# Loads of the scan's operands, issued half by half from the sync engine's queue instead of in one burst from GpSimd's

## The chip, the cores and the metric

One core of a Trainium2 chip runs the whole program. The metric is the device time of one execution in microseconds (us). Engines are called as in the profile: PE is TensorE (PEld its weight loads), DVE is VectorE, ACT is ScalarE, POOL is GpSimd, SP is SyncE, which only issues DMAs. The granted clock of PE is given as a share of 2.4 GHz: 1.00 is 2.4 GHz, 0.50 is 1.2 GHz.

## The reference, cut to what matters

The program is a two-layer network on 256 latent and 256 context tokens, 1024 channels wide, all in float32. Layer 0 mixes tokens by a recurrence (RWKV-7), layer 1 by attention; each mixer stands between two half feed-forward blocks. The change touches the recurrence alone:

```python
def rwkv_scan(state0, dd, reverse):
    def step(s, inp):
        r_t, w_t, k_t, v_t, a_t, b_t = inp
        sa = jnp.einsum('bhvk,bhk->bhv', s, a_t)
        s = s * w_t[:, :, None, :] + sa[..., None] * b_t[:, :, None, :] + v_t[..., None] * k_t[:, :, None, :]
        return s, jnp.einsum('bhvk,bhk->bhv', s, r_t)
```

It runs for 16 heads of 64 channels, forwards and backwards, over the context and then over the latent tokens.

## The kernel before, in words

The products of all layers are made of three passes (whi, wlo: each float32 operand is split in two), and fill most of the time. The scan is a stage of its own in the middle, from about 748 to 1134 us of the profiled execution. The stage before it (`rwkv_project`) has written its operands to DRAM for each of KT = 8 groups `ct` of two heads: `far` (the rates and receptances, read into the tile `ar`), `fbk` (the two sorts of keys, tile `bk`), `fv` (values, tile `v`), `fpc` (decays per chunk, tile `pc`), `fgl` and `bg` (for the readout). Tokens are cut into chunks of 64; a group has 8 chunks in each direction, in two halves `hf` of four.

A group goes through `produce` (scores of `ar` against `bk`, line 949, tile `scp`, masked by DVE into `sc`; `keys`, which transposes `bk` on PE, line 993, tile `btp`; `values`, line 973, tile `vtp`), `solve` (a triangular inverse on DVE), `couple` (64 and 32 small matmuls at a time, lines 1050, 1072 and 1089, tile `cpl`), `scan` (the recurrence over chunks, lines 1152 to 1197) and `readout` (lines 1213 to 1249).

The order is written out by hand. Time is counted in hops; a group starts every P = 24 hops, and at `t` hops after its own start a group does what the table `plan` says: `FILL` gives the pieces of `produce` (s is a score, k a key, v a value; the first digit is the half), `SOLVE` 14, `COUPLE` 30 to 40, `SCAN` from 41. So in every period of 24 hops PE does scores (hops 0 to 5), the couple of the group before (6 to 16), keys and values (15 to 23), all with scan steps between. `tc.manual_schedule()` keeps each engine to this order of emission.

The loads are issued from POOL's queue (`ldq = nc.gpsimd`). Group c loads for group c + 1 at `BK=(6, 9)`: `pc`, `ar` and `bk` of half 0 and of half 1, 512 KB for each `ar` or `bk`; its own `v`, 256 KB a half, at `V=(8, 14)`. `load_scan` at hops 30 and 42 reads `ax` and `r` out of `far` again, in pieces of 256 bytes, and the readout loads `ldgl` and `ldbg`. POOL issues in order, and does little else. `ar` and `v` have two buffers (pool `e2`), one for each half; `bk` has four (pool `m4`), so two for each half. The first group's `ar` and `bk` are loaded from SP before the loop.

Each engine's own instructions come by DMA as well: the profile's queue 8 (kind "instruction") brings 16 KB at a time.

Of the kernel before, what the change touches and what calls it, by code (L numbers as in the profile page):

```python
# [8 lines left out]
F32 = mybir.dt.float32  # L9
# [8 lines left out]
KT = 8  # L18
# [46 lines left out]
def drain(*gens):  # L65
    for g in gens:
        for _ in g:
            pass
# [19 lines left out]
class Net:  # L88


    def __init__(self, ctx, tc, a):
        self.ctx, self.tc, self.nc, self.a = ctx, tc, tc.nc, a
        self.last = {}
        self.plan = dict(
            P=24, SOLVE=14, RATE=5, COUPLE=range(30, 41), SCAN=41,
            FILL={0: ("s000", "s001"), 1: ("s010",), 2: ("s011",), 3: ("s100", "s101"), 4: ("s110",), 5: ("s111",), 15: ("k00",),
                  16: ("v00",), 17: ("v01",), 19: ("k01",), 20: ("k10",), 21: ("k11",), 22: ("v10",), 23: ("v11",)},
            END={(0, 0): (5, (3, 3)), (0, 1): (5, (3, 3)), (1, 0): (5, (3, 3))}, WO=(4, 4), NI=(5, 5),
            FST=(1, 3), WAIT=16, RH=0, FB=16, CLEAR=(14, 18), AS=1, BK=(6, 9), V=(8, 14), LOADS=(30, 42), SS=(6, 18), BC=(10, 22))
        nc = self.nc  # L100
        self.res = ctx.enter_context(tc.tile_pool(name="res", bufs=1))
        self.dram = ctx.enter_context(tc.tile_pool(name="dram", bufs=1, space=DRAM))
        self.vec = self.res.tile([128, NV, KT], F32, name="vec")
        self.cst = self.res.tile([128, NC], F32, name="cst")
        self.ones = self.res.tile([128, 128], F32, name="ones")
        cv = self.res.tile([128, KT, 2], F32, name="cv")
        self.cs = self.res.tile([128, KT, 32], F32, name="cs")
        self.mod = [self.res.tile([128, NMOD, KT, 2], F32, name=f"mod{l}") for l in range(2)]
        self.epsn = self.res.tile([128, 1], F32, name="epsn")
        self.epsg = self.res.tile([128, 1], F32, name="epsg")  # L110
        self.xsp = self.dram.tile([128, 2, KT, CTX], F32, name="xsp")
        nc.sync.dma_start(out=cv, in_=a["cv"])
        nc.sync.dma_start(out=self.vec, in_=a["vec"])
        nc.sync.dma_start(out=self.cst, in_=a["cst"])
        nc.vector.memset(self.epsg, GN_EPS)
        nc.vector.memset(self.ones, 1.0)
        nc.vector.memset(self.epsn, EPS)
        nc.vector.memset(self.cs, 0.0)
        nc.scalar.activation(out=self.cs[:, :, 0:2], in_=cv, func=AF.Silu)
# [19 lines left out]
    def mods01(self, b):  # L139
# [3 lines left out]
        for k4 in range(4):  # L143
            pool = self.first if k4 in self.plan["FST"] else self.wraw
            w = pool.tile([128, 2, 4, 128], F32, tag="mw" if pool is self.first else "raw", name="mw")
# [740 lines left out]
    def rwkv_scan(self):  # L886
        nc, a, tc = self.nc, self.a, self.tc
        with ExitStack() as st:
            def pool(nm, n, **kw):
                return st.enter_context(tc.tile_pool(name=nm, bufs=n, **kw))  # L890

            e2 = pool("e2", 2)
            l2 = pool("l2", 2)
            m3, m1, m2, m4, m5 = (pool(f"m{i}", i) for i in (3, 1, 2, 4, 5))
# [3 lines left out]
            idn = cst[:, C_ID:C_ID + 128]  # L898
            mask = cst[:, C_MK:C_MK + 128].unsqueeze(1).to_broadcast([128, 4, 128])

            def load(ct, hf, ldq=nc.gpsimd):

                z = zs.setdefault(ct, {})
                if hf == 0:
                    z["pc"] = m5.tile([128, 2, 8], F32, tag="pc", name="pc")
                    ldq.dma_start(out=z["pc"], in_=self.fpc[ct])
                z["bk", hf] = m4.tile([128, 2, 4, 128], F32, tag="bk", name="bk")
                z["ar", hf] = e2.tile([128, 2, 4, 2, 64], F32, tag="ar", name="ar")
                ldq.dma_start(out=z["ar", hf].rearrange("p d c s i -> p (d c s i)"), in_=self.far[ct, :, hf].rearrange("p d x -> p (d x)"))
                ldq.dma_start(  # L910
                    out=z["bk", hf].rearrange("p d c x -> p (d c x)"), in_=self.fbk[ct, :, hf].rearrange("p c s i -> p (c s i)"))

            def load_v(ct, hf):
                z = zs[ct]
                z["v", hf] = e2.tile([128, 2, 4, 64], F32, tag="v", name="v")
                ldq.dma_start(out=z["v", hf], in_=self.fv[ct, :, hf].rearrange("p d (c i) -> p d c i", c=4))

            def load_scan(ct, hf):

                z = zs[ct]  # L920
                src = self.far[ct, :, hf].rearrange("p d (c s i) -> p d c s i", c=4, s=2)
                ax = z["ax", hf] = axs[hf]
                for h in range(2):
                    q = 64 * h
                    ldq.dma_start(
                        out=ax[q:q + 64].rearrange("p d c s i -> p (d c) s i")[:, :, 1 - h],
                        in_=src[q:q + 64].rearrange("p d c s i -> p (d c) s i")[:, :, 0])
                z["r", hf] = m2.tile([128, 2, 4, 64], F32, tag="r", name="r")
                ldq.dma_start(out=z["r", hf], in_=src[:, :, :, 1])
# [321 lines left out]
            zs, reads = {}, []  # L1251
            ldq = nc.gpsimd
# [9 lines left out]
            def clear(t, n):  # L1262
                nc.scalar.activation(
                    out=t.rearrange("p a b c -> p (a b c)" if n == 2048 else "p a b c d -> p (a b c d)").rearrange("p (a b) -> p a b", b=128),
                    in_=self.ones.unsqueeze(1).to_broadcast([128, n // 128, 128]), func=AF.Copy, scale=0.0)

            def adv(g, n=1):
                for _ in range(n):
                    try:
                        next(g)  # L1270
                    except StopIteration:
                        return False
                return True

            pl = self.plan
            live = []
            load(0, 0, nc.sync)
            load(0, 1, nc.sync)
            hop, P = 0, pl["P"]
            while hop < P * KT or live or reads:  # L1280
                ct, o = hop // P, hop % P
                if hop in pl["CLEAR"]:
                    i = pl["CLEAR"].index(hop)
                    clear(axs[i], 1024)
                    clear(tts[i], 2048)
                if o == 0 and ct < KT:
                    live.append([hop, ct, produce(ct), solve(ct), couple(ct), scan(ct)])
                for z in reversed(live[:]):
                    if hop - z[0] >= pl["SCAN"] and not adv(z[5]):
                        live.remove(z)  # L1290
                for t0, c, pr, so, co, sn in live:
                    t, z = hop - t0, zs[c]
                    late = list(z.get("late", ()))
                    if late:
                        z["late"].clear()
                    for f in late:
                        f()
                    if pl["SOLVE"] <= t < pl["COUPLE"][0]:
                        for _ in range(pl["RATE"]):
                            if next(so, True):  # L1300
                                break
                    if t == pl["COUPLE"][0]:
                        drain(so)
                    if t in pl["COUPLE"]:
                        adv(co)
                    for nm in pl["FILL"].get(t, ()):
                        pr(nm)
                    for hf in range(2):
                        if t == pl["BK"][hf] and c + 1 < KT:
                            load(c + 1, hf)  # L1310
                        if t == pl["V"][hf]:
                            load_v(c, hf)
                        if t == pl["LOADS"][hf]:
                            load_scan(c, hf)
                reads[:] = [g for g in reads if adv(g)]
                hop += 1
# [279 lines left out]
```

## Time and profile before

| | us |
|---|---|
| median of three runs | 2381.75 (2378.70 to 2394.33) |
| the profiled execution | 2379.8 |
| its span, first to last instruction | 2377.7 |
| PE busy | 2186.2 (92%) |
| DVE busy | 1515.8 (64%) |
| ACT busy | 1073.8 (45%) |
| POOL busy | 181.8 (8%) |

The span is the stretch from the first to the last instruction; 2.1 us of the execution's time lie around it. The groups below come from that one execution; their times count from the start of the span. The scan's periods can be told by the first score matmul (line 949) of each group, at 776.34, 810.44, 852.95, 896.99, 940.75, 985.56 and 1032.16 us for groups 1 to 7. In each period the stretch from the first `cpl` matmul to the `ss` matmuls of line 1225 is the couple, and what follows up to the next group's first score is the rest of keys and values.

### The profile page before, as it was taken

How to read it: one execution, taken by the hardware profiler on the slowest of the kernel's cores; microseconds unless marked ns; L12 is line 12 of the kernel's file. 1: busy time of each engine (PE TensorE's matmuls, PEld its weight loads, DVE VectorE, ACT ScalarE, POOL GpSimd, SP SyncE). 2: the span in 40 equal slices, each digit the busy share in tenths (PEclk: the TensorE clock that was granted, in tenths of full speed). 3: DMA queues.
4: the chain of work that ended last, by engine and by line, in shares of the span. 5: the costliest groups of instructions: out<-in, count | busy, mean ns of one | idle time of the engine just before them, and what ended most of it. 6: DMA issues, size and time to landing. Idle time of an engine off the chain costs nothing.

```text
span 2377.7 us, 44861 instructions
## 1 busy us (share of the span) xinstructions
PE 2186.2 (92%) x18548; PEld 1869.9 (79%) x18548; DVE 1515.8 (64%) x2609; ACT 1073.8 (45%) x1912; POOL 181.8 (8%) x273
## 2 busy tenths in 40 slices
PE   6999999888996789898899999999999999998997
PEld 4777889666674677677888788998878898678997
DVE  3798326576887666563689832479983367775554
ACT  3222235445884354454653222464222355555443
POOL 0000000000454223221000000000000000000000
PEclk9999999898997799889999999999999999798999
DMA  7677336442676433312567633567763364104664
GB/s 256 194 217 226 96 99 196 149 134 88 228 248 226 129 94 97 119 58 71 182 196 234 207 97 93 156 191 235 230 212 95 107 182 126 61 11 123 180 180 138
DMA packets 103051, 366.25 MB, mean 154 GB/s; under 512 B 13008, under 2 KB 15424, under 8 KB 100160
## 3 DMA queue, kind: packets, MB, share of 16 engines
q1 hardware_dynamic: 85536, 300.35, 40.7%
q0 software_dynamic: 17312, 63.05, 8.2%
q8 instruction: 145, 2.38, 0.4%
q14 instruction: 58, 0.48, 0.1%
HBM read 330.78 MB, written 32.57 MB: 153 GB/s over the span
## 4 chain that ended last, share of the span: by engine, by line
PE 49%; DVE 11%; ACT 6%; issue 6%; DMA 5%; POOL 0%; DVEq 0%; ACTq 0%; POOLq 0%
PE h L262 5%; PE h L260 5%; PE h L261 5%; PE yps L262 4%; PE yps L260 4%; PE yps L261 4%; DMA y<-in_modt 3%; DVE junk L214 3%; DVE wlo L253 2%; PE scp L949 1%; PE op L1460 1%; PE cpl L1050 1%; PE yo L262 1%; ACT whi L252 1%; PE yo L260 1%
## 5 line engine op out<-in xcount | busy, mean ns | idle before, releaser
L252 ACT ACTIVATE whi<-wp 128x1024 fp32r<-128x1024 f32 (+1 forms) x396 | 409.2, 1034 | 745.8 <-PE h L261 378.8
L253 DVE TENSOR_TENSOR wlo<-wp,whi 128x1024 fp32r<-128x1024 f32 (+1 forms) x396 | 471.5, 1191 | 384.8 <-ACT whi L252 382.1
L262 PE MATMUL h<-nh,wlo 128*128 128x512 f32 (+1 forms) x1520 | 526.4, 347 | 19.4 <-DVE wlo L253 19.3
L260 PE MATMUL h<-nh,whi 128*128 128x512 f32 (+1 forms) x1520 | 525.3, 346 | 7.8 <-ACT whi L252 6.3
L261 PE MATMUL h<-nh,whi 128*128 128x512 f32 (+1 forms) x1520 | 523.7, 345 | 0.0
L262 PEld LDWEIGHTS h<-nh,wlo 128*128 128x128 f32 x1520 | 291.0, 192 | 63.4 <-DVE wlo L253 29.5
L260 PEld LDWEIGHTS h<-nh,whi 128*128 128x128 f32 x1520 | 291.6, 192 | 42.1 <-ACT whi L252 7.9
L261 PEld LDWEIGHTS h<-nh,whi 128*128 128x128 f32 x1520 | 291.6, 192 | 33.8
L262 PE MATMUL yps<-hid,wlo 128*128 128x256 f32 (+1 forms) x1034 | 314.2, 304 | 1.9 <-DVE wlo L253 1.9
L260 PE MATMUL yps<-hid,whi 128*128 128x256 f32 (+1 forms) x1034 | 314.2, 304 | 0.0
L261 PE MATMUL yps<-hid,whi 128*128 128x256 f32 (+1 forms) x1034 | 313.9, 304 | 0.0
L262 PEld LDWEIGHTS yps<-hid,wlo 128*128 128x128 f32 x1034 | 197.5, 191 | 10.5 <-DVE wlo L253 2.7
L261 PEld LDWEIGHTS yps<-hid,whi 128*128 128x128 f32 x1034 | 197.5, 191 | 7.9
L260 PEld LDWEIGHTS yps<-hid,whi 128*128 128x128 f32 x1034 | 197.5, 191 | 7.9
L214 DVE SCALAR_TENSOR_TENSOR junk<-y 128x1024 bf16<-128x1024 f32 x144 | 176.0, 1222 | 19.8 <-DMA y<-in_modt 17.7
L405 DVE TENSOR_TENSOR gg<-s,h 128x512 f32<-128x512 f32 (+1 forms) x98 | 55.9, 570 | 93.9 <-PE h L262 91.9
L214 DVE SCALAR_TENSOR_TENSOR junk<-dw,cb 128x1024 bf16<-128x1024 f32 x80 | 97.8, 1223 | 16.0 <-DMA dw<-in_modt 11.7
L407 ACT ACTIVATE hid<-gg 128x512 fp32r<-128x512 f32 (+1 forms) x98 | 52.3, 534 | 109.7 <-DVE gg L405 109.5
L262 PE MATMUL pp<-hid,wlo 128*128 128x512 f32 x232 | 93.1, 403 | 7.6 <-DVE wlo L253 7.5
L260 PE MATMUL pp<-hid,whi 128*128 128x512 f32 x232 | 93.8, 404 | 3.7 <-ACT whi L252 3.7
L261 PE MATMUL pp<-hid,whi 128*128 128x512 f32 x232 | 92.0, 397 | 0.0
L260 PE MATMUL yo<-nh,whi 128*128 128x256 f32 x192 | 56.4, 294 | 6.5 <-ACT nh L252 3.8
(306 smaller groups left out, 3503.5 us busy)
## 6 DMA issues: line engine op xcount, KB each, us to landing
wp<-in_w SPq DMA_DIRECT2D x243, 512.0 KB, 3.6
wp<-in_w SPq DMA_DIRECT2D x94, 448.0 KB, 3.4
y<-in_modt SPq DMA_DIRECT2D x72, 512.0 KB, 4.4
dw<-in_modt SPq DMA_DIRECT2D x40, 512.0 KB, 4.2
wp<-in_wrkv SPq DMA_DIRECT2D x40, 512.0 KB, 3.8
mw<-in_modw SPq DMA_DIRECT2D x32, 512.0 KB, 4.5
far<-ar POOLq DMA_DIRECT2D x8, 1024.0 KB, 5.7
ar<-far POOLq DMA_DIRECT2D x14, 512.0 KB, 5.7
```

Of the source, the lines that this page charges most:

```text
L214: nc.vector.scalar_tensor_tensor(out=junk, in0=ws[i % len(ws)], scalar=1.0, in1=cb[:, s], op0=ALU.mult, op1=ALU.mult, accum_out=self.mod[l ...
L252: nc.scalar.activation(out=hi, in_=raw, func=AF.Copy)
L253: nc.vector.tensor_tensor(out=lo, in0=raw, in1=hi.bitcast(F32), op=ALU.subtract)
L260: nc.tensor.matmul(out=ps, lhsT=wh, rhs=vh, start=first and j == 0, stop=False)
L261: nc.tensor.matmul(out=ps, lhsT=wh, rhs=vl, start=False, stop=False)
L262: nc.tensor.matmul(out=ps, lhsT=wl, rhs=vh, start=False, stop=last and j == n - 1)
L405: nc.vector.tensor_tensor(out=gg, in0=s1, in1=ps[1], op=ALU.mult)
L407: nc.scalar.activation(out=hi, in_=gg, func=AF.Copy)
L949: nc.tensor.matmul(out=p[h][:, c], lhsT=bk[q:q + 64, d, c], rhs=ar[q:q + 64, d, c].rearrange("p s i -> p (s i)"), start=True, stop=True, t ...
L1050: nc.tensor.matmul(out=p[q:q + 32, u], lhsT=lhs(8 * hf + u, q), rhs=rhs[q:q + 32, 8 * hf + u], start=True, stop=True, tile_position=(q, q))
L1460: nc.tensor.matmul(out=self.op.rearrange("p g q -> p (g q)"), lhsT=v2[:, b, i, pr, e].rearrange("p f d -> p (f d)"), rhs=pt[:, b, j].rearr ...
```

## The change

`load` is cut into `load_ar` (with `pc`), `load_bk` and a `load_v` that works for the next group too. All three issue from SP. They are called at hops of their own: `ar` at 3 and 6, `bk` at 17 and 22, `v` at 20 and 24, each right behind the last PE instruction that reads the buffer of the same half. `bk` moves from the pool with four buffers to the one with two. In `FILL`, `k01` moves from hop 19 to 16, `v00` from 16 to 17 and `v01` from 17 to 19. Before the loop all of group 0, its values too, is loaded from SP. The source pattern of `bk` is written with three dimensions in place of two. `load_scan` and the readout's loads stay on POOL.

```diff
             FILL={0: ("s000", "s001"), 1: ("s010",), 2: ("s011",), 3: ("s100", "s101"), 4: ("s110",), 5: ("s111",), 15: ("k00",),
-                  16: ("v00",), 17: ("v01",), 19: ("k01",), 20: ("k10",), 21: ("k11",), 22: ("v10",), 23: ("v11",)},
+                  16: ("k01",), 17: ("v00",), 19: ("v01",), 20: ("k10",), 21: ("k11",), 22: ("v10",), 23: ("v11",)},
...
-            FST=(1, 3), WAIT=16, RH=0, FB=16, CLEAR=(14, 18), AS=1, BK=(6, 9), V=(8, 14), LOADS=(30, 42), SS=(6, 18), BC=(10, 22))
+            FST=(1, 3), WAIT=16, RH=0, FB=16, CLEAR=(14, 18), AS=1, AR=(3, 6), BK=(17, 22), V=(20, 24), LOADS=(30, 42), SS=(6, 18), BC=(10, 22))
...
-            def load(ct, hf, ldq=nc.gpsimd):
+            def load_ar(ct, hf):
 
                 z = zs.setdefault(ct, {})
                 if hf == 0:
                     z["pc"] = m5.tile([128, 2, 8], F32, tag="pc", name="pc")
-                    ldq.dma_start(out=z["pc"], in_=self.fpc[ct])
-                z["bk", hf] = m4.tile([128, 2, 4, 128], F32, tag="bk", name="bk")
+                    nc.sync.dma_start(out=z["pc"], in_=self.fpc[ct])
                 z["ar", hf] = e2.tile([128, 2, 4, 2, 64], F32, tag="ar", name="ar")
-                ldq.dma_start(out=z["ar", hf].rearrange("p d c s i -> p (d c s i)"), in_=self.far[ct, :, hf].rearrange("p d x -> p (d x)"))
-                ldq.dma_start(
-                    out=z["bk", hf].rearrange("p d c x -> p (d c x)"), in_=self.fbk[ct, :, hf].rearrange("p c s i -> p (c s i)"))
+                nc.sync.dma_start(out=z["ar", hf].rearrange("p d c s i -> p (d c s i)"), in_=self.far[ct, :, hf].rearrange("p d x -> p (d x)"))
+
+            def load_bk(ct, hf):
+
+                z = zs[ct]
+                z["bk", hf] = e2.tile([128, 2, 4, 128], F32, tag="bk", name="bk")
+                nc.sync.dma_start(
+                    out=z["bk", hf].rearrange("p d c x -> p (d c x)"), in_=self.fbk[ct, :, hf].rearrange("p c s i -> p c (s i)"))
 
             def load_v(ct, hf):
                 z = zs[ct]
                 z["v", hf] = e2.tile([128, 2, 4, 64], F32, tag="v", name="v")
-                ldq.dma_start(out=z["v", hf], in_=self.fv[ct, :, hf].rearrange("p d (c i) -> p d c i", c=4))
+                nc.sync.dma_start(out=z["v", hf], in_=self.fv[ct, :, hf].rearrange("p d (c i) -> p d c i", c=4))
...
-            load(0, 0, nc.sync)
-            load(0, 1, nc.sync)
+            for hf in range(2):
+                load_ar(0, hf)
+                load_bk(0, hf)
+            for hf in range(2):
+                load_v(0, hf)
...
                     for hf in range(2):
-                        if t == pl["BK"][hf] and c + 1 < KT:
-                            load(c + 1, hf)
-                        if t == pl["V"][hf]:
-                            load_v(c, hf)
+                        for nm, f in (("AR", load_ar), ("BK", load_bk), ("V", load_v)):
+                            if t == pl[nm][hf] and c + 1 < KT:
+                                f(c + 1, hf)
                         if t == pl["LOADS"][hf]:
                             load_scan(c, hf)
```

## Rows read from the trace of the kernel before

**Rows 1.** Who waited for whom, PE, periods 2 to 6 (total, times, longest).
```profile
PE cpl L1050 <- issue: 14.9, 7, 4.5
...
PE up L1170 <- issue: 3.6, 1, 3.6
PE sp L1179 <- issue: 2.8, 1, 2.8
```

**Rows 2.** The same view, PE, period 1.
```profile
PE cpl L1050 <- issue: 6.4, 2, 5.1
PE cpl L1072 <- issue: 1.8, 1, 1.8
```

**Rows 3.** Timeline of PE in period 3 (idle time before, releaser).
```profile
872.95 0.33 PE L1050 MATMUL cpl<-td,qt 32*32 32x32 f32 x8 [4.45 <-issue]
...
874.88 1.08 PE L1050 MATMUL cpl<-td,qt 32*32 32x32 f32 x64
```

**Rows 4.** Timeline of POOL in period 3.
```profile
856.67 1.39 POOL L925 DMA_DIRECT2D ax<-far  x2 [12.66 <-PE rp L1159]
...
859.48 0.55 POOL L909 DMA_DIRECT2D ar<-far  x1
...
863.10 0.54 POOL L916 DMA_DIRECT2D v<-fv  x1
```

**Rows 5.** DMA queues, 868 to 870 us (packets, MB, share of 16 engines).
```profile
q0 software_dynamic: 235, 0.81, 101.1%
```

**Rows 6.** DMA queues, 870 to 872 us.
```profile
q0 software_dynamic: 79, 0.21, 30.4%
q8 instruction: 1, 0.02, 3.3%
```

**Rows 7.** Couple, groups 1 to 6: PE, PEld, DVE, ACT, POOL busy, PEclk, DMA, GB/s.
```profile
864.53:887.83 23.30, 17.14 (x593) 14.56 (x589) 9.55 (x19) 9.78 (x27) 5.81 (x10) 0.85 0.35 119
822.03:843.80 21.77, 17.32 (x589) 14.69 (x589) 9.54 (x19) 9.71 (x27) 5.75 (x10) 0.84 0.37 125
997.14:1019.20 22.06, 16.58 (x592) 14.09 (x589) 9.42 (x19) 9.79 (x27) 5.81 (x10) 0.92 0.39 131
1043.74:1063.17 19.43, 15.49 (x593) 13.18 (x589) 9.43 (x19) 9.79 (x27) 4.35 (x7) 1.00 0.12 31
908.57:931.60 23.03, 17.78 (x593) 15.03 (x589) 9.55 (x19) 9.80 (x27) 5.84 (x10) 0.85 0.36 126
952.33:976.40 24.07, 17.98 (x593) 15.41 (x589) 9.54 (x19) 9.79 (x27) 5.83 (x10) 0.79 0.32 113
```

**Rows 8.** Keys and values after the couple, periods 3, 6 and 7.
```profile
887.83:896.99 9.16, 8.83 (x171) 7.66 (x169) 8.14 (x32) 5.88 (x17) 0.21 (x1) 1.00 0.14 47
1019.20:1032.16 12.96, 12.96 (x173) 11.09 (x169) 10.27 (x39) 5.88 (x17) 0.22 (x1) 0.60 0.09 32
1063.17:1074.71 11.54, 11.54 (x172) 9.99 (x168) 10.24 (x40) 5.88 (x17) 0.21 (x1) 0.70 0.11 38
```

**Rows 9.** All of period 1, same columns.
```profile
776.34:810.44 34.10, 24.36 (x664) 21.94 (x662) 22.66 (x63) 12.19 (x29) 8.75 (x15) 0.71 0.36 106
```

**Rows 10.** Timeline of PE: last key of group 3, second half's score.
```profile
892.07 0.71 PE L993 MATMUL btp<-cst,bk 64*128 64x64 f32 x8
...
901.73 1.16 PE L949 MATMUL scp<-ar,bk 64*128 64x128 f32 x16
```

**Rows 11.** Tile bk: time from issue to landing.
```profile
DMA to landing us min/median/max: 3.2/7.3/11.4
```

**Rows 12.** DMA issues of the scan (KB each, median us to landing).
```profile
r<-far POOLq DMA_DIRECT2D x16, 256.0 KB, 4.6
```

**Rows 13.** Timeline of PE, group 0's values.
```profile
769.82 1.98 PE L973 MATMUL vtp<-cst,v 128*64 128x64 f32 x32 [4.66 <-DMA v<-fv]
```

**Rows 14.** The chain that ended last, period 1 (start, us, what).
```profile
779.35 1.04 DVE td L1031
```

**Rows 15.** Timeline of SP, after the start of the scan.
```profile
1074.59 1.50 SPq L266 DMA_DIRECT2D wp<-in_wrkv  x3
```

## The prediction

> **What bounds the kernel now.** The change is confined to the scan, so I read that stage alone. First the chain of waits of PE, the busiest engine there. In periods 2 to 6 its largest entries have no releaser that the profile shows ("issue"): 14.9 + 3.6 + 2.8 = 21.3 us [rows 1], and 6.4 + 1.8 = 8.2 us in period 1 [rows 2]. No row there waits for `ar`, `bk` or `v`, so in the steady periods the loads are already hidden, and the change cannot gain by bringing data sooner. The reader should then ask what an engine waits for when it waits for nothing: its instructions. In period 3 PE stands still for 4.45 us and resumes at 872.95 [rows 3]. Between 868 and 870 us POOL's queue alone fills all 16 DMA engines (101.1%) and no instruction packet is among the transfers [rows 5]; between 870 and 872 the load falls to 30.4% and one instruction packet comes through [rows 6]; PE goes on a microsecond or two later. The filled engines are the burst: POOL issues `ax` and `r` from 856.67, the two sets of `ar`, `bk` and `v` from 859.48 to 863.10 [rows 4], 2 x (512 + 512 + 256) KB in some 4 us, and the readout's loads behind them. The couple right after it is the place where PE uses up instructions fastest, 64 tiny matmuls in about a microsecond. So a fetch that queues behind the burst stops PE.
>
> Next, the couple by stretch [rows 7]. With the burst in front it takes 21.77, 23.30, 23.03, 24.07 and 22.06 us in periods 2 to 6. In period 7, where no next group's `ar` and `bk` are loaded, it takes 19.43 us with the same 593 matmuls, at a granted clock of 1.00 (2.4 GHz) against 0.79 to 0.92. There the burst's price can be read without a model: part is standing still, part is the clock, which is at half speed (0.50, 1.2 GHz) right after a long stop (64 `cpl` matmuls take 1.08 us there [rows 3]).
>
> **The change part by part.**
>
> *The burst goes.* In each period 2.5 MB leave the stretch just ahead of the couple; of these `ar` comes back at hops 3 and 6 (2 x 512 KB), `bk` and `v` at 17 to 24, behind the couple. What stays on POOL ahead of the couple is `ax`, `r`, `ldgl`, `ldbg`. Period 7 has the same on POOL with two `v` loads (512 KB) and is the nearest row. At 19.43 us in each of periods 2 to 6 the sum is (21.77 + 23.30 + 23.03 + 24.07 + 22.06) - 5 x 19.43 = 114.23 - 97.15 = 17.1 us. The second `ar`, issued after the last score and so close to the couple, is 512 KB that period 7 has not; I leave 0.5 us a period for it and take 14.6 us. Bounds: 0, if the fetches are slow for a reason of their own, and 17.1 us. A couple much below 19.43 us is not expected, since period 7 still loses 19.43 - 15.49 = 3.9 us of PE's time with the DMA engines 12% busy.
>
> *Period 1.* It takes 34.10 us at a clock of 0.71 [rows 9], and 8.2 us of it are stops of this kind [rows 2]. Its couple runs alone on PE, so a fetch is more easily the bound even on free DMA engines. I take 5 us, bounds 0 and 8.2.
>
> *The clock behind the couple.* Keys and values take 9.16 us at full clock (period 3; three more periods are the same within 0.1), but 12.96 and 11.54 in periods 6 and 7, where the clock is at half speed for part of them [rows 8]. Period 7 shows that this can come without a stop in the couple. Whether it does I cannot derive from the rows: two of six now. I take two of six again, 0 us. Bounds: none of six gives (12.96 - 9.16) + (11.54 - 9.16) = 6.2 us; all six, at 11.54, cost 6 x 2.38 - 6.2 = 8.1 us.
>
> *`bk` in single buffers.* Now the four buffers let it load a whole period early. Afterwards the second half's load may be issued only when the last key matmuls have read it, at 892.07 + 0.71 = 892.8 us in period 3, and must have landed for the score at 901.73 [rows 10]: 8.9 us. The first half has about as much or more, from hop 16 to 24. From issue to landing `bk` takes 3.2 to 11.4 us now, median 7.3 [rows 11], the long ones inside the burst. The new three-dimensional pattern might be carried in pieces of 512 bytes; the nearest row is `r`, in pieces of 256 bytes, 4.6 us for half the bytes [rows 12], so 9.2 us at most by doubling. In that stretch DMA moves 47 GB/s at a share of 0.14 [rows 8], so I take a landing under 6 us and a wait of 0; bounds 0 and (9.2 - 8.9) x 7 = 2 us.
>
> *Queues.* POOL loses some fifty issues of about 0.55 us [rows 4], but it idles 12.66 us before `ax` alone; that gives nothing. SP takes them on. It waits there for PE at each load, in the order of the hops, and what is queued behind are the next stage's weights, issued at 1074.59 [rows 15] after the last `v` load, which leaves at about 1033 us. Nobody waits for that. If SP were late all the same, the first to notice would be the score of the second half, as above.
>
> *The start.* Group 0's values are loaded ahead, so the 4.66 us that PE waits for them [rows 13] can go. What ends this stretch is DVE's inverse, done at 779.35 [rows 14], well after those matmuls, so I take 0; bounds -4.7 and, if 512 KB more delay the first scores, as much the other way. The three moved `FILL` entries are the same instructions in another order among hops that nobody waits on: 0.
>
> The sum: 14.6 + 5 = 19.6 us, 2379.8 - 19.6 = 2360 us for an execution like the profiled one, which is 2 us below the median of the three runs. I predict 2361.
>
> **The rivals.**
>
> *No gain: the fetch is slow by itself.* PE uses instructions faster in the couple than they can be fetched, and the burst only happens at the same time. For it: period 7 keeps a stop or two with free DMA engines. Against it: its couple is 2.3 to 4.6 us shorter, and the packet of rows 6 came only as the burst drained [rows 5 and 6]. Time: 2380 us, at most 3 from it. The Trainium skill, page "DMA: Bandwidth & Descriptors", section "Queues, rings and completion order", says that a DMA engine goes round the queue rows that have work, packet by packet; by that rule a fetch would pass between two packets of the burst and the time would be this rival's. The trace speaks against it: no fetch among 235 packets in 2 us, beside a PE that stands still.
>
> *Given back by the clock.* The couple gets its 14.6 us, but PE's quiet moments in keys and values fall so that the clock drops in all six periods: 19.6 - 8.1 = 11.5 us, 2368 us. For it: periods 6 and 7. Against: four of six did not drop.
>
> *Slower: `bk` lands late.* Each period waits for the second half, and the wait stands on the path, since scores feed everything after. The price is 7 x (L - 8.9) us for a landing time L; it eats the gain from L = 8.9 + 19.6 / 7 = 11.7 us and at 14 us gives 2379.8 - 19.6 + 35.7 = 2396 us. For it: 11.4 us have been seen. Against: only in the burst, which is gone, and with 0.14 of the DMA engines' time taken where these loads now run.
>
> **How the numbers follow.** Chances: the forecast 0.65 (2348 to 2368), no gain 0.17 (2377 to 2383), given back by the clock 0.09 (around 2368), slower 0.09 (2380 to 2400). The forecast's own best case is 17.1 + 8.2 + 6.2 = 31.5 us, 2348. The range runs from there to 2383, where the no-gain case ends; what lies beyond is most of the slower case and a little below. One per cent is 23.8 us, about what a measurement of this kernel can tell from no change: faster by more means under 2358. The forecast's middle lies 3 us above that line, so a little over half of its 0.65 goes to "within": faster 0.36, within 0.55 with the no-gain case, the clock's and part of the slower one's, slower 0.09.
>
> **What would show each step.** Right: in periods 2 to 6 the couple stretch at about 20 us, PE's stops by "issue" from 21.3 to about 13 us in sum, instruction packets about 4 us apart in the couple and none late, and clock 1.00 there. The second score of a half never waits for DMA `bk`, and `bk` lands in under 6 us. POOL's queue shows only `ax`, `r`, `ldgl`, `ldbg`. Wrong: stops of 3 to 5 us that remain with free DMA engines (the no-gain rival); a clock of 0.6 to 0.7 in all stretches of keys and values; a row of PE's waits that names `bk` or `ar`; or a second `ar` and `ax` that fill the DMA engines as the burst did. Off in size only: period 1, where I had no undisturbed period to compare with.

## The result and the profile after

The changed kernel takes 2356.11 us (median of four, 2353.81 to 2361.63), the kernel before beside it 2383.32 us (median of four, 2378.70 to 2394.33): a ratio of 0.9883, interval 0.9844 to 0.9922. A second series (e5 below) gave 2352.44 against 2379.28 us, 0.9896 (0.9866 to 0.9925). The time forecast was 2361; the gain is a little over 1% (by its interval 0.8 to 1.6%), where I had given "within 1%" the larger chance. The profiled execution took 2353.81 us, with a span of 2351.9 (before 2379.8 and 2377.7).

PE's waits in the kernel after; the first two lines are periods 2 to 6 and answer to [rows 1], the last two period 1, answering to [rows 2]:

```profile
PE cpl L1054 <- issue: 8.2, 7, 2.0
...
PE up L1174 <- issue: 0.7, 1, 0.7
...
PE scp L953 <- DMA bk<-fbk: 7.3, 2, 6.3
PE cpl L1054 <- issue: 3.2, 2, 1.9
```

The stops (the waits without a releaser, "issue" in the profile) fall from 21.3 to 8.9 us, the longest from 4.5 to 2.0; I had expected about 13. In period 1 there is a new first line: PE waits for `bk`.

The stretches of the kernel after: the couples of groups 1 to 6 in order of time, answering to [rows 7], then keys and values of periods 3, 5 and 6, answering to [rows 8]; same columns:

```profile
812.23:830.33 18.10, 16.28 (x585) 13.98 (x581) 9.64 (x20) 10.29 (x28) 4.57 (x7) 0.95 0.19 57
852.55:875.07 22.52, 21.19 (x585) 18.26 (x581) 10.64 (x21) 10.39 (x28) 4.55 (x7) 0.65 0.16 48
897.13:915.64 18.51, 16.31 (x585) 13.99 (x581) 9.64 (x20) 10.29 (x28) 4.56 (x7) 0.95 0.20 59
937.88:957.90 20.02, 16.97 (x584) 14.34 (x580) 9.54 (x19) 10.23 (x28) 4.34 (x7) 0.91 0.17 50
978.64:998.26 19.62, 16.48 (x585) 14.13 (x581) 9.86 (x20) 10.36 (x28) 4.55 (x7) 0.94 0.18 53
1023.01:1040.31 17.30, 15.69 (x585) 13.27 (x581) 9.42 (x19) 10.23 (x28) 4.33 (x7) 1.00 0.13 35
...
875.07:885.55 10.48, 10.48 (x179) 9.46 (x177) 9.08 (x37) 5.25 (x16) 0.00 (x0) 0.78 0.44 144
957.90:967.05 9.15, 8.52 (x180) 7.48 (x176) 8.13 (x32) 5.43 (x17) 0.22 (x1) 1.00 0.59 180
998.26:1011.42 13.16, 13.16 (x179) 11.72 (x177) 9.77 (x38) 5.39 (x16) 0.00 (x0) 0.58 0.35 119
```

Four of the five couples take 18 to 20 us with the DMA engines busy 0.16 to 0.20 of the time, where it was 0.32 to 0.39. The second takes 22.52 us for another reason: PE's busy time has risen to 21.19 us at a clock of 0.65, so it did not stand still, it ran slowly. Keys and values now hold the data traffic (0.35 to 0.59 in the three stretches shown), and most of them are longer than the 9.15 us of a stretch at full clock.

Where the loads now run: SP's and then POOL's timeline of period 5 in the kernel after (start, duration), answering to [rows 4]:

```profile
930.78 4.68 SPq L908 DMA_DIRECT2D ar<-far  x2
956.30 0.32 SPq L914 DMA_DIRECT2D bk<-fbk  x1
```

```profile
930.01 1.39 POOL L929 DMA_DIRECT2D ax<-far  x2 [14.40 <-PE rp L1163]
931.39 0.90 POOL L933 DMA_DIRECT2D r<-far  x1
```

And what the couple's fetches find: DMA queues of the kernel after in 8.5 us of a couple, 898 to 906.5 us, then the same length in the kernel before, from 865.5 to 874 us:

```profile
q1 hardware_dynamic: 34, 0.10, 3.1%
q8 instruction: 3, 0.05, 2.0%
```

```profile
q0 software_dynamic: 580, 1.96, 59.9%
q8 instruction: 1, 0.02, 0.8%
```

Three instruction packets pass in the time in which one did. The first 4 us of a couple show the difference best: period 3 of the kernel before, period 4 of the kernel after (columns as in [rows 7]; the DMA share is the last number but one):

```profile
864.53:868.53 4.00, 3.49 (x220) 3.12 (x217) 0.96 (x3) 0.95 (x5) 1.47 (x3) 1.00 0.98 345
```

```profile
897.13:901.13 4.00, 3.27 (x195) 2.85 (x193) 0.96 (x3) 0.53 (x3) 0.00 (x0) 1.00 0.27 102
```

That queue 8 carries PE's instructions, and that PE waits for them, can be read from all twelve profiles of this case together. In periods 1 to 6 PE has 113 stops longer than 0.6 us; 107 of them end 1.2 to 1.7 us after a packet of queue 8 has landed. The other six are the same 1.29 us ahead of the first couple matmul of period 1, 7 to 15 us after the last such packet, so they are waits for something else.

### The profile page after: what moved, and what is told of

It reads as the page before. It is cut to its first block, busy times and chain, and to the rows that moved or that the text cites. A ratio compares the mean times of both kernels' runs of the same rounds, so it can differ in the third digit from the quotient of the medians.

```text
span 2351.9 us, 44901 instructions
## 1 busy us (share of the span) xinstructions
PE 2185.8 (93%) x18548; PEld 1872.4 (80%) x18548; DVE 1516.4 (64%) x2609; ACT 1074.2 (46%) x1912; POOL 155.1 (7%) x222
## 4 chain that ended last, share of the span: by engine, by line
PE 52%; DVE 10%; issue 5%; ACT 5%; DMA 4%; POOL 1%; DVEq 0%; ACTq 0%; POOLq 0%
PE h L262 6%; PE h L260 6%; PE h L261 6%; PE yps L262 4%; PE yps L260 4%; PE yps L261 4%; DMA y<-in_modt 3%; DVE junk L214 2%; DVE wlo L253 2%; PE scp L953 1%; PE op L1466 1%; PE cpl L1054 1%; PE sp L1190 1%; DMA fgl<-yx 1%; PE up L1174 1%
## 5 line engine op out<-in xcount | busy, mean ns | idle before, releaser
L214 DVE SCALAR_TENSOR_TENSOR junk<-dw,cb 128x1024 bf16<-128x1024 f32 x80 | 97.9, 1223 | 14.8 <-DMA dw<-in_modt 10.8
L407 ACT ACTIVATE hid<-gg 128x512 fp32r<-128x512 f32 (+1 forms) x98 | 52.3, 534 | 108.4 <-DVE gg L405 108.2
```

Source lines behind the costliest of these rows:

```text
L214: nc.vector.scalar_tensor_tensor(out=junk, in0=ws[i % len(ws)], scalar=1.0, in1=cb[:, s], op0=ALU.mult, op1=ALU.mult, accum_out=self.mod[l ...
L407: nc.scalar.activation(out=hi, in_=gg, func=AF.Copy)
```

## The experiments

Two more profiles of the kernel before and one more of the changed kernel come first, because one profiled execution of this kernel differs from another by more than some terms of the sum.

**The kernel before, twice more (e9, e10).** No edit.

> The kernel before, profiled once more, for what lies outside the scan: in the two profiles of the changed kernel the scan's stage starts 5 to 6 us earlier than in the one profile of the kernel before, though nothing there is changed. Chance of the clock: its scan starts anywhere from 751 to 762 us here too, its stops in periods 2 to 6 come to 15 to 23 us and the scan's stage is as long as before within 6 us. An effect of the change outside the scan: it starts at 758 to 760 us again.

> The same kernel once more, the same two readings: a start of the scan between 751 and 762 us and stops of 15 to 23 us in periods 2 to 6 if the difference outside the scan is chance, 758 to 760 us if it is the change's.

Measured: 2382.64 and 2366.97 us, beside one run of the same kernel of 2383.86. Their stops by issue in periods 2 to 6 are 21.5 and 20.5 us, beside 21.3 in the first profile, so the stops are no accident of one execution. Their scans begin at 757.8 and 756.7 us: within the range for chance, but so close to the other reading's 758 to 760 that they do not decide between the two. The scan, from the first score to the last readout, takes 374.5, 379.0 and 368.2 us in the three profiles. A difference of 5 us between two single profiles therefore tells nothing.

**The changed kernel again (e5).** No edit.

> The changed kernel once more, beside the kernel before on the same chip. Theory: a ratio of 0.985 to 0.993; in its profile stops by issue of 7 to 12 us in periods 2 to 6 and the scan's stage 14 to 22 us shorter than in the kernel before; what lies outside the scan differs by a few us either way from one profile to the next. Rival, part of the gain lies outside the scan and is the change's too (other places in memory, other order): the stage before the scan ends 4 to 6 us earlier than in the kernel before in this profile as well.

Measured: the ratio of 0.9896 given above. Scan 362.5 us (first profile 356.4), stops 11.0 us (8.9), five couples of 18.58, 19.59, 18.61, 25.85 and 19.28 us. The fourth again has a low clock, 0.62, now in period 5.

**The burst left whole, from SP's queue (e2).** The kernel before with only the queue changed:

```
-            def load(ct, hf, ldq=nc.gpsimd):
+            def load(ct, hf, ldq=nc.sync):
...
-                ldq.dma_start(out=z["v", hf], ...
+                nc.sync.dma_start(out=z["v", hf], ...
```

> The kernel before with its burst at the old hours and four buffers of bk, issued from SP in place of POOL. Theory, the hour counts: the instruction packets wait as before, stops by issue 15 to 23 us in periods 2 to 6, couple 21 to 24 us, time within 7 us of the kernel before. Rival, the queue counts: couple 18 to 20 us, stops 7 to 13 us, time 15 to 28 us under before.

Measured: 2384.72 against 2377.44 us, 1.0034 (0.9994 to 1.0074). PE's waits of this kernel, periods 2 to 6:

```profile
PE cpl L1050 <- issue: 14.3, 6, 3.8
PE up L1170 <- issue: 3.5, 1, 3.5
```

With 1.2 us in a third row the stops come to 19.0 us; SP's queue by itself gives nothing. The Trainium skill, page "DMA: Bandwidth & Descriptors", section "Issuing engines are not separate DMA queues", says that DMAs end on the same 16 DMA engines whichever engine started them; this run agrees.

**The new hours, from POOL's queue (e1).** The changed kernel with `load_ar`, `load_bk` and `load_v` on POOL, group 0 left on SP:

```
-            def load_ar(ct, hf):
+            def load_ar(ct, hf, q=nc.gpsimd):
...
-                nc.sync.dma_start(out=z["ar", hf]...
+                q.dma_start(out=z["ar", hf]...
```

> The changed kernel with its new hours and single buffers, but the loads of groups 1 to 7 issued from POOL as before (group 0 from SP). Theory, the hour counts: the burst is gone here too, so the couple takes 18 to 20 us in periods 2 to 6 on average (period 3 of the changed kernel aside, whose clock was low), PE's stops by issue in periods 2 to 6 come to 7 to 13 us, and the time is 15 to 28 us under the kernel before. Rival, the queue counts (SP's queue leaves room for instruction packets and POOL's does not): the couple stays at 22 to 24 us, the stops at 18 us or more, the time within 6 us of before.

Measured: 2372.62 against 2377.44 us, 0.9966 (0.9932 to 1.0000); stops 14.7 us. So the hours alone, on POOL, bring about 5 us at most. Two signs came out as the rival (the queue counts) had them: the time is within 6 us of before, and the five couples average 22.8 us. But the stops lie between the two readings, and e2 has shown that the queue by itself gives nothing. POOL's timeline of this kernel ahead of the couple of period 3 resolves it (idle time before, and who ended it):

```profile
852.41 0.54 POOL L906 DMA_DIRECT2D pc<-fpc  x1
856.49 0.53 POOL L908 DMA_DIRECT2D ar<-far  x1 [3.55 <-PE scp L953]
857.02 0.71 POOL L1217 DMA_DIRECT2D ldgl<-fgl  x1
857.72 0.56 POOL L1219 DMA_DIRECT2D ldbg<-bg  x1
858.28 1.40 POOL L929 DMA_DIRECT2D ax<-far  x2
859.67 0.89 POOL L933 DMA_DIRECT2D r<-far  x1
860.85 0.56 POOL L908 DMA_DIRECT2D ar<-far  x1 [0.29 <-PE scp L953]
861.41 0.70 POOL L1217 DMA_DIRECT2D ldgl<-fgl  x1
```

POOL works in order. While it waits 3.55 us until PE has read the single buffer of `ar`, the readout's `ldgl` and `ldbg` stand behind it; then two sets of them, two `ar`, `ax` and `r` leave together within 6 us, and a smaller burst meets the couple, which begins at 863.3:

```profile
863.32:867.32 4.00, 3.43 (x220) 3.03 (x217) 0.96 (x3) 1.44 (x5) 0.50 (x1) 1.00 0.75 242
```

In all five couples the DMA engines are busy for 0.67 to 0.89 of the first 4 us, and two of the couples run at a clock of 0.63 and 0.64. As this trace reads, moving the loads to SP is of use because it takes these waits off POOL.

**Traffic put back ahead of the couple (e3, e7).** The changed kernel, which reads 2 MB a period more from `fbk` into a tile that nobody uses (no computation is left out), at the hours of `ar` (e3); and half of it at the second hour alone (e7, whose condition has `hf == 1 and` in front):

```
+                        if t == pl["AR"][hf] and c + 1 < KT:
+                            for _ in range(2):
+                                dm = m4.tile([128, 1024], F32, tag="dm", name="dm")
+                                nc.sync.dma_start(out=dm, in_=self.fbk[c, :, hf].rearrange("p c s i -> p (c s i)"))
```

> The changed kernel with four more loads of 512 KB in each of periods 0 to 6, two behind each load of ar, into tiles that nobody reads: the 2 MB that the change had taken away from the stretch ahead of the couple are put back, from SP. Theory, a fetch of instructions waits behind what fills the DMA engines: stops by issue return to 15 to 25 us in periods 2 to 6, the couple to 21 to 25 us, and the time lies 12 to 28 us above the changed kernel, so between 15 us under and 5 us over the kernel before. Rival, the gain came from something else in the change (single buffers, queue, order of keys and values): the time stays within 5 us of the changed kernel, some 20 to 30 us under before.

> The changed kernel with two more loads of 512 KB in each period behind the second load of ar, just ahead of the couple, into tiles that nobody reads. Theory, the hour counts: stops by issue in periods 2 to 6 of 14 to 20 us, the couple 1 to 3 us longer each, the time 5 to 15 us above the changed kernel. Rival, the amount counts: equal to the half dose behind the couple within 4 us.

Measured: e3 2383.30 against 2377.44 us, 1.0013 (0.9974 to 1.0053), stops 21.4 us. e7 2376.13 against 2379.28 us, 0.9980 (0.9954 to 1.0007), stops 15.7 us. Two MB ahead of the couple undo the whole gain, one MB most of it: some 24 us against e8 below, where I had expected 5 to 15. DMA queues of e7 from 907 to 911 us, at the start of the couple of period 4, where PE then stands still for 3.06 us until 913.33:

```profile
q1 hardware_dynamic: 400, 1.47, 93.3%
...
q8 instruction: 1, 0.02, 1.6%
```

The one instruction packet starts at 910.87, when the loads are nearly done. The couples of e7, periods 2 to 6:

```profile
817.84:839.37 21.53, 17.51 (x585) 14.77 (x581) 9.53 (x19) 10.22 (x28) 4.36 (x7) 0.84 0.29 95
860.10:885.39 25.29, 22.40 (x585) 19.22 (x581) 10.62 (x21) 10.38 (x28) 4.55 (x7) 0.62 0.25 87
907.58:933.74 26.16, 22.61 (x584) 19.27 (x580) 10.62 (x21) 10.38 (x28) 4.56 (x7) 0.63 0.24 84
958.50:978.24 19.74, 16.98 (x585) 14.30 (x581) 9.54 (x19) 10.23 (x28) 4.34 (x7) 0.91 0.30 105
998.98:1025.64 26.66, 22.21 (x584) 19.08 (x580) 10.62 (x21) 10.38 (x28) 4.54 (x7) 0.64 0.24 81
```

Three of them are at a low clock, so in this profile the dose costs more by slow running than by standing still.

**The same traffic behind the couple (e4, e8).** Two MB at the second hour of `bk` (e4), or 1 MB at the first (e8, with `hf == 0` and `range(2)`):

```
+                        if hf == 1 and t == pl["BK"][hf] and c + 1 < KT:
+                            for _ in range(4):
...
```

> The same four loads of 512 KB, all behind the second load of bk (hop 22), so that they run while keys and values are at work and not ahead of the couple. Theory, only the hour of the traffic counts: within 5 us of the changed kernel, stops by issue in periods 2 to 6 at 7 to 13 us. Rival, the amount of traffic counts wherever it runs: as slow as the early dose, 12 us or more above the changed kernel.

> The same two loads behind the first load of bk (hop 17). The late dose of 2 MB ran on into the next group's scores and held back ax, r and ar there, so it was not late enough to tell; 1 MB at hop 17 ends before the scores. Theory, the hour counts: stops as in the changed kernel, 7 to 12 us, time within 4 us of it. Rival, the amount counts: as the half dose ahead of the couple.

Measured: e8 2352.21 against 2379.28 us, 0.9898 (0.9865 to 0.9930), the ratio of the changed kernel beside it; stops 10.8 us. The couples of e8, periods 2, 3 and 6:

```profile
824.04:842.67 18.63, 16.43 (x584) 14.02 (x580) 9.64 (x20) 10.29 (x28) 4.57 (x7) 0.95 0.19 53
864.87:884.74 19.87, 16.88 (x585) 14.32 (x581) 9.55 (x19) 10.23 (x28) 4.34 (x7) 0.91 0.17 50
...
987.66:1007.15 19.49, 16.49 (x584) 14.14 (x580) 9.86 (x20) 10.37 (x28) 4.57 (x7) 0.93 0.18 55
```

e7 and e8 move the same megabyte and were timed beside each other: at one hour it takes away some 24 us, at the other nothing. So it is the hour, not the amount. e4 did less well: 2359.64 against 2377.44 us, 0.9937 (0.9897 to 0.9977), with stops of 15.9 us. Its 2 MB were not late enough to be a clean test. Four of them leave SP from 934.91, late in period 4, and land after:

```profile
DMA to landing us min/median/max: 5.3/7.4/9.6
```

The scores of period 5 begin at 939.61; `ar`, `ax` and `r` are pushed back and land until 955, inside the couple that begins at 951.19, where PE stands still for 2.33 us. The traffic went behind one couple and pushed other loads ahead of the next.

**`ar` too behind the couple (e6).** The changed kernel with

```
-AR=(3, 6), BK=(17, 22)
+AR=(18, 21), BK=(17, 22)
...
-                z = zs[ct]
+                z = zs.setdefault(ct, {})
```

> The changed kernel with the loads of ar at hops 18 and 21, so behind bk and v on SP and behind the couple; only ax, r and the readout's loads are left ahead of it. Theory, what fills the DMA engines ahead of the couple holds the instructions back: stops by issue in periods 2 to 6 fall from 9 to 2 to 6 us, the couple to 17 to 18.5 us at full clock, and the time is 3 to 10 us under the changed kernel. Rival one, the rest of the stops is the speed of fetching itself: as the changed kernel within 3 us. Rival two, slower: bk of the second half now comes behind 2 MB more or less at once and lands late; a row in PE's waits names bk or ar, and each microsecond of it costs 7 us.

Measured: 2351.19 against 2379.28 us, 0.9891 (0.9856 to 0.9927). Its couples, periods 2 to 4:

```profile
815.78:833.84 18.06, 15.64 (x585) 13.25 (x581) 9.42 (x19) 10.22 (x28) 4.35 (x7) 1.00 0.15 39
854.58:871.86 17.28, 16.04 (x585) 13.66 (x581) 9.63 (x20) 10.27 (x28) 4.56 (x7) 0.95 0.16 45
894.17:912.55 18.38, 15.98 (x584) 13.37 (x580) 9.43 (x19) 10.22 (x28) 4.34 (x7) 1.00 0.14 36
```

Stops fall once more, to 7.1 us, and this profile's scan is the shortest of all, 351.7 us; the median cannot be told from the changed kernel's 2352.44, as rival one had it. So `ar`, left ahead of the couple, costs little, and what stops remain with it gone are not its doing. In period 1 PE now waits 5.7 us for `ar` and 4.6 for `bk`.

**All runs together.** One number nearly orders them: the DMA engines' busy share in the first 4 us of the couples, mean of periods 2 to 6 (a packet counts where it starts, so a share can pass 1).

| kernel | DMA share | stops (us) |
|---|---|---|
| before (first profile) | 0.99 | 21.3 |
| e2 | 1.03 | 19.0 |
| e3 | 1.02 | 21.4 |
| e7 | 0.87 | 15.7 |
| e1 | 0.77 | 14.7 |
| e4 | 0.52 | 15.9 |
| changed (first, e5), e8 | 0.21 to 0.22 | 8.9 to 11.0 |
| e6 | 0.01 | 7.1 |

In the 4 us ahead of the couple the changed kernel fills the engines as much as ever (1.02 to 1.05, against 0.82 to 0.94 before). So, by these rows, what counts is not that loads run ahead of the couple, but how much of them still runs once it has begun.

## Why the prediction was right, and where its sizes were off

The sums below compare means, of three profiles of the kernel before (the first, e9, e10) and two of the changed one (the first, e5).

**The burst: right.** I took 14.6 us off the couples of periods 2 to 6. They took 114.2, 116.6 and 112.4 us before, mean 114.4, and 98.8 and 101.9 after, mean 100.3: -14.1 us. In the couple at 897.13 the first fetch came as the loads ended, and PE waited 0.73 us for it; the later ones followed every 3.4 to 4.2 us. That the held fetch is the cause is shown from both sides: put back, the traffic restores the stops (e3, e7); put elsewhere, it costs nothing (e8).

That the size fits so well is in part luck. Period 7 was a long measure: its 19.43 us were 18.10 and 17.82 in e9 and e10, and 17.30 and 17.84 after. And "clock 1.00 there", my sign for the couple, was wrong: in the first profile after the clock is 0.95, 0.65, 0.95, 0.91 and 0.94. One couple in fifteen before (e9, period 6: 26.92 us at 0.62) and two in ten after ran at 0.62 to 0.65. Without these a couple takes 22.6 us before and 19.0 after, which would be -17.8 us for five; the slow couples, for which the sum had no term, give 3.7 of that back. A sign of being wrong that I had named, loads of `ar` and `ax` that fill the DMA engines as the burst did, did come about ahead of the couple (1.02 to 1.05), and the gain came all the same, since they end as it begins.

**The start and period 1: right mechanism, size off.** From the first score to the beginning of period 2 it took 51.3, 52.5 and 51.1 us, mean 51.6, and takes 47.3 and 50.1, mean 48.7: -2.9 us, where I took 5 (bounds 0 and 8.2). The stops there fell from 8.2 to 3.6 us in the first profiles. I had read all 8.2 as waits for instructions, but 1.3 us of it, which both kernels have, come 7.3 and 11.7 us after the last instruction packet: 6.9 us before and 2.4 after were of that kind.

**The clock behind the couple: the step that failed.** I took 0 us, two of six stretches slow as before. Keys and values of periods 2 to 6 took 49.6, 47.9 and 49.6 us, mean 49.0, and take 54.1 and 52.3, mean 53.2: +4.2 us, inside my bounds (-6.2 to 8.1). One of five was slow in each profile of before; four and three of five are now. So the rival "given back by the clock" has happened by half, beside the forecast and not in place of it. Why more of them are slow is not shown: the loads now run there, and `FILL` was changed too; e6 and e8 have three slow ones in five as well, e1 two.

**`bk` in single buffers: right in the steady periods, wrong in period 1.** Landing times of `bk` in the kernel after, groups 2 to 7:

```profile
DMA to landing us min/median/max: 3.6/4.0/5.7
```

Under 6 us, as taken, against 3.2/7.3/11.4 [rows 11], and no row of periods 2 to 6 waits for it; there the rival of the late `bk` falls. But group 1's two loads land after 9.2 and 12.1 us (8.0 and 11.7 in e5), as late as that rival had it, and period 1, which I had not looked at for this, waits 7.3 us for them (6.9 in e5), since in group 0 nothing but short hops lies between the load and its use. What hides it is DVE's inverse. The chain that ended last, kernel after (start, us):

```profile
774.49 1.04 DVE td L1035
775.53 2.91 DVE sc L958 x5
```

In the kernel before the same step follows `td` [rows 14]:

```profile
780.39 2.91 DVE sc L954 x5
```

In both, the five score reads, of the same length, follow `td` at once; the wait was over before. From the first score, `td` starts after 20.3 to 21.4 us in the three profiles before and 21.1 and 21.5 us after, so the start term of 0 holds as well.

**No gain, the fetch is slow by itself: falls, but for a rest.** The 9 to 11 us of stops that remain, and the 7.1 of e6, are what is true of it. The Trainium skill says that a DMA engine goes round the queue rows packet by packet (page "DMA: Bandwidth & Descriptors", section "Queues, rings and completion order"). What I drew from it, that a fetch would pass between two packets of the burst, is not borne out here: in e7, 400 packets of one queue took 93.3% of the 16 engines, and the fetch came as they ended. Whether the rule itself is at fault is not shown, since no run here tells whether the profile's packets are the ones that the rule counts. Nor is the hold a strict one: in the kernel before an instruction packet got through at 864.38 us, with the burst taking 89.3% of the engines (864 to 866 us).

**The sum.** First score to second period -2.9, couples -14.1, keys and values +4.2, period 7's couple -0.9 (18.4 to 17.6), the rest of the scan -0.7: -14.4 us, from 373.9 to 359.5. I had forecast -19.6; the parts that fell short are period 1 and the clock. The spans of the same profiles differ by 20.4 us (2374.5 to 2354.1): the scan begins at 757.8 us before (mean) and 753.4 after, and what follows it is 1.7 us shorter. The code of these stretches is unchanged but for the loads of group 0, for which the first score waits as long as before (11.5 to 12.0 us before, 11.7 and 11.4 after), and other kernels that share it scatter likewise (first score at 753.2 in e7, 754.1 in e6, 759.0 in e1, 761.7 in e8). That my time comes so near the measured one thus owes something to parts that I had not counted, and is to that extent luck; where those 6 us in the spans, and the 7 us more in the medians, come from stays open.

## What to carry to other kernels

A row of waits without a releaser, on an engine that issues many tiny instructions, can be a wait for instructions: look in the DMA queues for the instruction packet that ends it, and for what fills the DMA engines just ahead of it. Then see to it that the bulk loads have landed when that stretch begins, or start behind it; moving them to another queue at the same hour gave nothing here. And follow where they push the next loads. A load with a single buffer is best issued from an engine whose in-order queue holds nothing that others wait for, and its first group must be looked at by itself, since there the steady deadlines don't hold.

## What was not expected of the hardware

A couple can run at half speed for most of its length, with no long stop ahead of it. In the first profile of the changed kernel, PE stops for 1.33 us in period 3, and from 859.18 to the couple's end at 875.07 it is busy without a gap at a clock of 0.50; the couple is 4 us longer than its neighbours. In e7 such a stretch follows a stop of 3.06 us: the rest of that couple, 913.33 to 933.74 us, is at 0.52, close to the lower level of 1.2 GHz. The stop of 4.45 us in the kernel before had given no such stretch [rows 3, 7]. The change did not bring these couples about: the kernel before has one in e9, where a stop of 4.03 us falls into it. Which periods are hit changes from run to run (period 3, then period 5 of the same kernel; three couples in e7, none in e8). What decides it is open, and was not tried.

Fetches that nothing holds are still a limit. They come 3.4 to 4.2 us apart, each brings 16 KB, and PE resumes about 1.4 us after one has landed (packet landed at 911.89, PE on again at 913.33 in e7). With the DMA engines all but idle in the couple's first 4 us, e6 still keeps 7.1 us of stops in five periods. The changed kernel's profile has 146 such packets for 37,096 matmuls and weight loads, so one brings some 254 of them, and the 585 + 581 of a couple need 4.6 packets. At 3.4 us each that is some 16 us, an estimate from these counts; the couples at a clock of 1.00 take 17.3 to 18.6 us in the kernels with the new hours.
